# Two modulation matrices loaded in half-width pieces through two buffers

## The chip, the cores and the metric

The kernel runs on one core of one Trainium2 chip. The metric is the device time of one launch in microseconds (us); smaller is better. Engines are named as the profile names them: PE is TensorE (PEld its weight loads), DVE VectorE, ACT ScalarE, POOL GpSimd, SP the queue that issues most DMA loads.

## What is computed

Two transformer blocks run over the same 256 tokens of width 1024. Only the first block's beginning matters here: one vector `c` makes six modulation vectors of 1024 columns by one product with a 1024 x 6144 matrix `ada_w`, and these scale and shift the tokens around the mixer and the mixture of experts.

```python
mod = (jax.nn.silu(c.astype(F32)) @ ada_w.astype(F32) + ada_b.astype(F32)).astype(x.dtype)
sh1, sc1, g1, sh2, sc2, g2 = [m[:, None, :] for m in jnp.split(mod, 6, axis=-1)]
h = rms_norm(x, norm1_g) * (1 + sc1) + sh1
z = h @ w_in
...
attn = dsa_sparse_attention(hs(q), hs(k), hs(v), iq.reshape(B, S, IDX_HEADS, IDX_DIM), ik, iw, rel_bias)
rw = rwkv7_branch(zr, ...)
mixed = jax.nn.sigmoid(ga) * (attn @ w_attn_br) + jax.nn.sigmoid(gr) * (rw @ w_rwkv_br)
x = x + g1 * (mixed @ w_out)
h2 = rms_norm(x, norm2_g) * (1 + sc2) + sh2
x = x + g2 * moe_ffn(h2, ...)
```

## The kernel before

The program is one stream of work for one core, in stages: the first mixer (until about 345 us), the mixture of experts (until about 950 us), and the second block (until the end). A scheduler sets the order of the instructions on every engine, from priorities and from a model of durations of its own; on the chip each engine then runs its queue strictly in that order, and an instruction that waits holds up all behind it. A DMA issue on SP waits there, too.

`modulation(K, g, ...)` makes the modulation vectors in three groups `g` of 2048 columns. Each group runs over eight steps `k` of 128 rows of `ada_w`: a load of 128 x 2048 numbers (1024 KB, 8 KB for each partition), then four products, one for each quarter `q` of 512 columns. The moving side is 512 columns of the weights, the stationary side is `c` copied to 32 columns, and the four quarters go to rows 0, 32, 64 and 96 of one PSUM bank (`mod`), so that the four products lie side by side in the array. In the trace each of them is two records. After eight steps DVE adds the bias (L919, out to the tile `modr`).

Group 0 is needed at once and runs at the start through the wide ring of weight tiles. Groups 1 and 2 are needed only near the end of the mixer. `first_mixer` issues them behind the projection of the rwkv inputs, inside `K.later(400)`, which sets their priorities back, so that they fill in between other work. Their loads have a pool of their own, `ada`, with one buffer `adaw` of 8 KB per partition: the load of step k+1 can be issued only when the last product of step k has read the buffer.

Around them run, on PE: the dense projections of the mixer (`dense_T` and `dense_tok`, three products for each pair of tiles, L186 to L188, weights `w` from `in_w_in_dram` through a ring of three tiles, loaded by L142 and split into a high and a low part by ACT L152 and DVE L153); the chunked rwkv recurrence in two halves (`rwkv`: L1145, L1156, L1133, L1193 to L1271), a long chain between PE, ACT and DVE; the indexer's scores (`dsa_choose`: L1317, read by ACT L1320); and the attention over chosen keys (`dsa`: L543, L583, L555). Sigmoid gates (L1432, L1438) close the mixer, and then the output projections with `w_rwkv_br`, `w_attn_br` and `w_out` follow. ACT loads a function table when it changes between sigmoid and exponential.

Of the kernel before, what the change touches and what calls it, by code (L numbers as in the profile page):

```python
# [893 lines left out]
def modulation(K, g, pool, wpool=None):  # L894

    nc, a = K.nc, K.a
    if g == 0:
        sc = K.t([128, 8], "silc")
        nc.scalar.activation(sc, K.cc["c"], AF.Sigmoid)
        nc.vector.tensor_mul(sc, sc, K.cc["c"])  # L900
        K.c32 = K.t([128, 8, 32], "c32")
        nc.vector.tensor_copy(K.c32, sc[:, :, None].to_broadcast([128, 8, 32]))
        K.modr, K.mrow = {}, {}
    mb = K.modr[g] = K.t([128, 512], "modr", 2, pool=pool)
    v = a["ada_b"][0, g * 2048:g * 2048 + 2048]
    nc.scalar.dma_start(mb, bass.AP(v.tensor, v.offset, [[512, 4], [0, 32], [1, 512]]))
    b = K.bank("mod")
    for k in range(8):
        if g == 0:
            w = K.wtile()  # L910
        else:
            w = K.t([128, 2048], "adaw", pool=wpool)
        nc.sync.dma_start(w, a["ada_w"][0, k * 128:k * 128 + 128, g * 2048:g * 2048 + 2048])
        for q in range(4):
            nc.tensor.matmul(b[32 * q:32 * q + 32], K.c32[:, k], w[:, q * 512:q * 512 + 512], start=(k == 0),
                             stop=(k == 7), skip_group_check=True)
        if k < 7:
            yield
    nc.vector.tensor_add(mb, b, mb)  # L919
    if g:  # L920
        K.mrow[g] = K.dram.tile([4, 512], F32, name="modrow%d" % g)
        nc.scalar.dma_start(K.mrow[g], K.modr[g].rearrange("(q r) n -> q r n", r=32)[:, 0])
    yield
# [436 lines left out]
def first_mixer(K):  # L1360
# [8 lines left out]
    for i, _ in enumerate(modulation(K, 0, first)):  # L1369
        if i == 3:  # L1370
            nc.sync.dma_start(K.X, a["x"][0].rearrange("(h p) d -> p h d", p=128))
# [3 lines left out]
    with K.scope("p1in"):  # L1375
# [20 lines left out]
        with K.later(400), K.after(K.ACT):  # L1396
            for g in (1, 2):
                for _ in modulation(K, g, first, adap):
                    pass
            with K.stream(pool=first, tmp="mod"):  # L1400
                router_in(K, first)
# [752 lines left out]
```

## Time and profile before

| | before |
|---|---|
| median of 3 runs | 1708.5 us (1707.46 to 1713.28) |
| the profiled execution | 1706.39 us, of which the span from first to last instruction is 1704.4 us |
| PE busy | 1620.0 us, 95% of the span |
| DVE, ACT, POOL busy | 829.3, 644.9, 84.8 us |
| mean granted TensorE clock | 0.981 of full speed |
| loads of `adaw` | 16 of 1024 KB, issued from 91.7 to 227.7 us |
| products on `adaw` | 128 records, from 97.8 to 234.5 us |

A line of the time line of an engine gives the start, the length, the engine, the line of the kernel, the operation, the tiles (out<-in), the shape, and how many equal instructions in a row it stands for; in brackets stands the idle time before it and what ended it. Records of matmuls overlap, since they are pipelined: what one costs is read from the start of the next.

### The profile page before, as it was taken

The numbers are of one execution on the slowest core, as the hardware profiler recorded it, in microseconds if no ns is written. First come the engines' busy times: TensorE is split into PE (matmuls) and PEld (weight loads), VectorE is DVE, ScalarE is ACT, GpSimd is POOL, SyncE is SP. The second block draws the span as 40 slices with busy tenths as digits, with TensorE's granted clock in tenths as the row PEclk, the third lists the DMA queues.
The fourth block names the chain that finished last, engine by engine and source line by source line (L and its number), as shares of the span: only waits on it lengthen the run. The fifth ranks groups of instructions, "written<-read, shape, count | busy, mean of one in ns | idle before, by whom it ended". The sixth has DMA issues, their size and how long they took to land. (4 is left out here: it accounts for less than half of the span.)

```text
span 1704.4 us, 28908 instructions
## 1 busy us (share of the span) xinstructions
PE 1620.0 (95%) x11910; PEld 1234.2 (72%) x11910; DVE 829.3 (49%) x1534; ACT 644.9 (38%) x1093; POOL 84.8 (5%) x105
## 2 busy tenths in 40 slices
PE   5999999998989999999999899999999999999997
PEld 2967667786547565557665587889998876989996
DVE  2664786676211321211211356666555677665554
ACT  2432444553121111120111347565444455554443
POOL 2000000103000000000000111211000000000000
PEclk9989899999999999999999999999999999999999
DMA  9454651774999999999999652546555533445551
GB/s 357 151 198 149 206 173 52 276 293 166 414 417 411 390 402 413 412 414 411 393 416 410 198 173 96 191 154 201 193 181 196 175 125 106 143 154 191 197 182 55
DMA packets 138321, 419.06 MB, mean 246 GB/s; under 512 B 10666, under 2 KB 17588, under 8 KB 118732
## 3 DMA queue, kind: packets, MB, share of 16 engines
q1 hardware_dynamic: 126272, 396.39, 62.5%
q0 software_dynamic: 4336, 12.34, 2.2%
q10 hardware_dynamic: 7580, 8.47, 1.7%
q8 instruction: 94, 1.54, 0.4%
q14 instruction: 39, 0.32, 0.1%
HBM read 410.88 MB, written 6.32 MB: 245 GB/s over the span
## 5 line engine op out<-in xcount | busy, mean ns | idle before, releaser
L153 DVE TENSOR_TENSOR w<-w 128x1024 fp32r<-128x1024 f32 (+1 forms) x283 | 347.5, 1229 | 260.8 <-ACT w L152 260.0
L152 ACT ACTIVATE w<-w 128x1024 fp32r<-128x1024 f32 (+1 forms) x285 | 299.9, 1054 | 315.7 <-PE acc L188 223.4
L1897 PE MATMUL tmp<-w 128*32 128x256 f32 (+2 forms) x2560 | 202.1, 396 | 14.9 <-DMA w<-in_exp_up_dram 10.0
L1897 PEld LDWEIGHTS tmp<-w 128*32 128x32 f32 (+2 forms) x2560 | 120.6, 122 | 87.4 <-DMA w<-in_exp_up_dram 13.3
L188 PE MATMUL acc<-hTh,w 128*128 128x256 f32 (+2 forms) x552 | 159.4, 289 | 1.1 <-DVE w L153 1.1
L186 PE MATMUL acc<-hTh,w 128*128 128x256 f32 (+2 forms) x552 | 158.0, 287 | 1.8 <-ACT w L152 1.1
L187 PE MATMUL acc<-hTl,w 128*128 128x256 f32 (+2 forms) x552 | 159.0, 288 | 0.2 <-DVE hTl L153 0.2
L186 PE MATMUL tmp<-hTh,w 128*128 128x256 f32 x512 | 143.6, 280 | 0.0
L187 PE MATMUL tmp<-hTl,w 128*128 128x256 f32 x512 | 143.0, 279 | 0.0
L188 PE MATMUL tmp<-hTh,w 128*128 128x256 f32 x512 | 142.9, 279 | 0.0
L188 PEld LDWEIGHTS acc<-hTh,w 128*128 128x128 f32 (+1 forms) x552 | 105.5, 191 | 6.6 <-issue 4.6
L187 PEld LDWEIGHTS acc<-hTl,w 128*128 128x128 f32 (+1 forms) x552 | 105.7, 192 | 5.1 <-issue 4.1
L186 PEld LDWEIGHTS acc<-hTh,w 128*128 128x128 f32 (+1 forms) x552 | 105.7, 192 | 4.7 <-issue 2.0
L1925 PE MATMUL tmp<-w,fT 128*32 128x512 f32 (+2 forms) x640 | 105.2, 597 | 0.5 <-ACT fT L1913 0.5
L186 PE MATMUL acc<-w,gh 128*128 128x512 f32 x256 | 100.0, 390 | 0.0
L188 PE MATMUL acc<-w,gl 128*128 128x512 f32 x256 | 99.8, 390 | 0.0
L187 PE MATMUL acc<-w,gh 128*128 128x512 f32 x256 | 99.6, 389 | 0.0
L186 PEld LDWEIGHTS tmp<-hTh,w 128*128 128x128 f32 x512 | 96.1, 188 | 0.5
L188 PEld LDWEIGHTS tmp<-hTh,w 128*128 128x128 f32 x512 | 96.3, 188 | 0.0
L187 PEld LDWEIGHTS tmp<-hTl,w 128*128 128x128 f32 x512 | 95.8, 187 | 0.5
L1903 DVE SCALAR_TENSOR_TENSOR ff<-tmp,gsl,fs 128x256 f32<-128x256 f32 x26 | 12.6, 483 | 171.6 <-ACT fs L1901 171.6
L1901 ACT ACTIVATE fs<-tmp 128x256 f32<-128x256 f32 x26 | 10.0, 385 | 217.9 <-PE tmp L1897 217.9
(625 smaller groups left out, 2884.4 us busy)
## 6 DMA issues: line engine op xcount, KB each, us to landing
w<-in_exp_gate_dram SPq DMA_DIRECT2D x64, 1024.0 KB, 18.2
w<-in_exp_up_dram SPq DMA_DIRECT2D x64, 1024.0 KB, 18.7
w<-in_exp_down_dram SPq DMA_DIRECT2D x64, 1024.0 KB, 15.4
w<-in_mlp_w_dram SPq DMA_DIRECT2D x64, 1024.0 KB, 5.2
w<-in_w_in_dram SPq DMA_DIRECT2D x23, 1024.0 KB, 6.2
adaw<-in_ada_w_dram SPq DMA_DIRECT2D x16, 1024.0 KB, 5.2
w<-in_xa_wkv_dram SPq DMA_DIRECT2D x16, 1024.0 KB, 20.5
w<-in_sb_w_in_dram SPq DMA_DIRECT2D x12, 1024.0 KB, 5.2
```

Of the source, the lines that this page charges most:

```text
L152: self.nc.scalar.activation(hi, src, AF.Copy)
L153: self.sub.tensor_tensor(lo, src, hi.bitcast(F32), op=OP.subtract)
L186: mm(out, lh, rh, start=first, stop=False, skip_group_check=True)
L187: mm(out, lh, rl, start=False, stop=False, skip_group_check=True)
L188: mm(out, ll, rh, start=False, stop=last, skip_group_check=True)
L1897: nc.tensor.matmul(b[at:at + w, x * 256:x * 256 + 256], X[:, k, i * 128 + at:i * 128 + at + w], d[n][:, k], start=(x == 0 and k == 0), sto ...
L1901: nc.scalar.activation(s, b[:, 0:256], AF.Silu)
L1903: nc.vector.scalar_tensor_tensor(f, b[:, 256:512], g, s, op0=OP.mult, op1=OP.mult)
L1925: nc.tensor.matmul(b[at:at + w], fT[:, k, at:at + w], d["exp_down"][:, k, n * 512:n * 512 + 512], start=(k == 0), stop=(k == 1), skip_grou ...
```

## The change

For groups 1 and 2 a step of 128 rows is cut into two halves of columns. There are 16 loads `i` for each group; `k` is the row step, `n` the half. A load brings columns `n*256` to `n*256 + 256` of each of the four quarters, 128 x 4 x 256 numbers (512 KB, four pieces of 1 KB for each partition). The pool `ada` now has two such buffers of 4 KB per partition, so its size stays as it was. Each half has four products of 256 columns into its half of the bank. Group 0 is as it was.

```diff
     b = K.bank("mod")
-    for k in range(8):
-        if g == 0:
-            w = K.wtile()
-        else:
-            w = K.t([128, 2048], "adaw", pool=wpool)
+    for i in range(16 if g else 0):
+
+        k, n = divmod(i, 2)
+        c = slice(n * 256, n * 256 + 256)
+        w = K.t([128, 4, 256], "adaw", 2, pool=wpool)
+        nc.sync.dma_start(w, a["ada_w"][0, k * 128:k * 128 + 128, g * 2048:g * 2048 + 2048]
+                          .rearrange("p (q c) -> p q c", q=4)[:, :, c])
+        for q in range(4):
+            nc.tensor.matmul(b[32 * q:32 * q + 32, c], K.c32[:, k], w[:, q], start=(i == 0), stop=(k == 7),
+                             skip_group_check=True)
+        yield
+    for k in range(0 if g else 8):
+        w = K.wtile()
         nc.sync.dma_start(w, a["ada_w"][0, k * 128:k * 128 + 128, g * 2048:g * 2048 + 2048])
```

Since the scheduler sets the order, the change moves more than its own lines. Lines behind the change have numbers higher by 8 in the changed kernel (L1133 is L1141, the products L915 are L916).

On the queue of SP, from the first load of `adaw` on, before (`w<-in_w_in_dram` are the weights of the projections):

```order
L913 DMA adaw<-in_ada_w_dram 128x2048 x2
L142 DMA w<-in_w_in_dram 128x4x512
L913 DMA adaw<-in_ada_w_dram 128x2048
L142 DMA w<-in_w_in_dram 128x4x512
L913 DMA adaw<-in_ada_w_dram 128x2048 x2
L142 DMA w<-in_w_in_dram 128x4x512
L913 DMA adaw<-in_ada_w_dram 128x2048 x3
L142 DMA w<-in_w_in_dram 128x4x512
```

and in the changed kernel, the whole of it:

```order
L913 DMA adaw<-in_ada_w_dram 128x4x256 x6
L142 DMA w<-in_w_in_dram 128x4x512
L913 DMA adaw<-in_ada_w_dram 128x4x256 x2
L142 DMA w<-in_w_in_dram 128x4x512
L913 DMA adaw<-in_ada_w_dram 128x4x256 x14
L142 DMA w<-in_w_in_dram 128x4x512
L913 DMA adaw<-in_ada_w_dram 128x4x256 x6
L142 DMA w<-in_w_in_dram 128x4x512
L913 DMA adaw<-in_ada_w_dram 128x4x256 x4
L142 DMA w<-in_w_in_dram 128x4x512 x8
```

Fourteen loads of `adaw` in a row now stand ahead of a load of projection weights, and the last load of `adaw` stands ahead of eight of them, where before it stood ahead of four.

On PE in the middle of the first rwkv half (L1133 are its 64 x 64 products), before:

```order
L1133 MATMUL rw<-rP,rWT 64x64 x8
L186 MATMUL acc<-hTh,w 128x256
L187 MATMUL acc<-hTl,w 128x256
L915 MATMUL mod<-adaw,c_104 32x512
L1133 MATMUL rw<-rWT,rP 64x64 x8
L1133 MATMUL rw<-rP,rWT 64x64 x8
L915 MATMUL mod<-adaw,c_104 32x512 x3
L188 MATMUL acc<-hTh,w 128x256
L186 MATMUL acc<-hTh,w 128x256
```

and at the same place in the changed kernel:

```order
L1141 MATMUL rw<-rP,rWT 64x64 x8
L916 MATMUL mod<-adaw,c_104 32x256 x4
L188 MATMUL acc<-hTh,w 128x256
L1141 MATMUL rw<-rWT,rP 64x64 x8
L1141 MATMUL rw<-rP,rWT 64x64 x8
L916 MATMUL mod<-adaw,c_104 32x256 x4
L186 MATMUL acc<-hTh,w 128x256
L1141 MATMUL rw<-rW,rlm 64x64 x16
L1141 MATMUL rw<-rWT,rP 64x64 x8
L1141 MATMUL rw<-rP,rWT 64x64 x8
L916 MATMUL mod<-adaw,c_104 32x256 x4
```

A half step now stands behind nearly every second run of rwkv products, and dense products that filled these places have moved back. Over the whole queue of PE the products on `adaw` stand in 38 runs, where they stood in 21, and the last of them stands right behind the indexer's scores instead of in the second rwkv half.

## Rows read from the trace of the kernel before

**Rows 1.** The page, busy time by engine and its share of the span.

```profile
PE 1620.0 (95%) x11910; PEld 1234.2 (72%) x11910; DVE 829.3 (49%) x1534; ACT 644.9 (38%) x1093; POOL 84.8 (5%) x105
```

**Rows 2.** Stretches: length, busy time of each engine (instructions), granted clock, DMA share, GB/s.

```profile
97.00:197.00 100.00, 94.62 (x986) 67.17 (x985) 58.90 (x133) 34.36 (x66) 2.04 (x2) 0.94 0.53 178
197.00:240.00 43.00, 41.57 (x234) 28.84 (x233) 38.84 (x102) 21.89 (x36) 0.00 (x0) 0.99 0.55 192
240.00:312.00 72.00, 71.67 (x779) 53.26 (x779) 51.42 (x130) 32.43 (x77) 6.03 (x9) 1.00 0.27 83
```

**Rows 3.** Groups of PE from 80 to 245 us: busy, mean ns, idle before.

```profile
L915 PE MATMUL mod<-adaw,c 128*32 128x512 f32 x128 | 23.1, 633 | 3.5 <-DMA adaw<-in_ada_w_dram 3.5
```

**Rows 4.** Time line of PE, products on adaw and those around them.

```profile
97.34 0.28 PE L186 MATMUL acc<-hTh,w 128*128 128x256 f32 x1
97.78 1.06 PE L915 MATMUL mod<-adaw,c 128*32 128x512 f32 x8 [0.16 <-DMA adaw<-in_ada_w_dram]
98.77 0.39 PE L187 MATMUL acc<-hTl,w 128*128 128x256 f32 x1
99.00 0.28 PE L188 MATMUL acc<-hTh,w 128*128 128x256 f32 x1
99.12 0.28 PE L186 MATMUL acc<-hTh,w 128*128 128x256 f32 x1
...
126.51 1.05 PE L915 MATMUL mod<-adaw,c 128*32 128x512 f32 x2
127.49 1.15 PE L1133 MATMUL rw<-rW,rlm 64*64 64x64 f32 x32
128.72 0.68 PE L1133 MATMUL rw<-rWT,rP 64*64 64x64 f32 x16
129.23 0.63 PE L1133 MATMUL rw<-rP,rWT 64*64 64x64 f32 x16
129.79 1.06 PE L915 MATMUL mod<-adaw,c 128*32 128x512 f32 x6
130.78 0.39 PE L186 MATMUL acc<-hTh,w 128*128 128x256 f32 x1
```

**Rows 5.** Time line of PE, the two other products on adaw that waited.

```profile
192.38 1.94 PE L915 MATMUL mod<-adaw,c 128*32 128x512 f32 x8 [2.29 <-DMA adaw<-in_ada_w_dram]
...
219.68 1.06 PE L915 MATMUL mod<-adaw,c 128*32 128x512 f32 x8 [1.08 <-DMA adaw<-in_ada_w_dram]
```

**Rows 6.** Time line of PE among the expert products, a run on 32 columns.

```profile
569.60 5.60 PE L1897 MATMUL tmp<-w 128*32 128x256 f32 x100
```

**Rows 7.** Time line of SP, issues of loads.

```profile
91.66 7.58 SPq L913 DMA_DIRECT2D adaw<-in_ada_w_dram  x2
...
135.77 0.38 SPq L142 DMA_DIRECT2D w<-in_w_in_dram  x1
...
184.28 10.42 SPq L913 DMA_DIRECT2D adaw<-in_ada_w_dram  x2
...
211.95 0.33 SPq L913 DMA_DIRECT2D adaw<-in_ada_w_dram  x1
```

**Rows 8.** Issues of two loads: engine, count, KB each, median us to landing.

```profile
adaw<-in_ada_w_dram SPq DMA_DIRECT2D x16, 1024.0 KB, 5.2
...
memx<-memkv ACTq DMA_DIRECT2D x16, 256.0 KB, 3.7
```

**Rows 9.** Stretches of 5 us around the longest wait; columns as in the second group.

```profile
185.00:190.00 5.00, 4.13 (x25) 2.12 (x22) 4.11 (x12) 3.58 (x9) 0.00 (x0) 0.79 1.04 361
190.00:195.00 5.00, 2.71 (x11) 0.70 (x10) 1.95 (x6) 2.24 (x4) 0.00 (x0) 0.50 0.22 65
195.00:200.00 5.00, 5.00 (x30) 4.61 (x29) 2.44 (x4) 1.98 (x4) 0.00 (x0) 0.69 0.60 210
```

**Rows 10.** Time line of PE: the values' projection begins, attention ends, w_rwkv_br begins.

```profile
203.74 0.39 PE L186 MATMUL acc<-w,hTh 128*128 128x512 f32 x1
203.97 0.39 PE L187 MATMUL acc<-w,hTh 128*128 128x512 f32 x1
...
307.46 0.86 PE L555 MATMUL tmp<-pT,av__232 128*64 128x256 f32 x6
...
329.11 0.40 PE L186 MATMUL acc<-w 128*128 128x512 f32 x1
```

**Rows 11.** Groups of ACT until 340 us, a table load.

```profile
L1432 ACT ACT_TABLE_LOAD x2 | 2.6, 1283 | 0.0
```

## The prediction

> **What bounds the kernel now.** I read the busy times first: PE is busy 95% of the span, the next engine 49% [rows 1]. Then the stretches in which groups 1 and 2 of the modulation run. From 97 to 197 us PE is busy 94.62 of 100 us, DVE 58.90; from 197 to 240 us PE 41.57 of 43 us and DVE 38.84, so there the two are nearly level; from 240 to 312 us PE 71.67 of 72 us [rows 2]. The stage is bound by PE's queue, which runs strictly in order, and time is saved or lost by what that queue holds and by what it waits for. The third view is the group of the products on `adaw`: 128 records, busy 23.1 us, and an idle time of only 3.5 us before them [rows 3]. That idle time is all that a second buffer can give back directly, 0.2% of the span. The waits behind it are three: 0.16 us at 97.78, 2.29 us at 192.38 and 1.08 us at 219.68 [rows 4, 5]. The issue queue shows why: the load after the products of one step is issued at once (184.28 and 211.95 us [rows 7]) and its products start 8.1 and 7.7 us later. At all other steps the scheduler has put enough other work between.
>
> **The change, part by part.** It removes nothing from the work: the same bytes are loaded and the same columns multiplied.
>
> First, the products. A whole step costs 0.99 us from its start to that of the next instruction (97.78 to 98.77). A quarter alone (two records) costs as much, 126.51 to 127.49, because the four quarters run side by side [rows 4]. For 256 columns on 32 rows of output the trace has the expert products: 100 records in 5.60 us, so eight in 0.45 us [rows 6]. Two halves are 0.90 us, and so 0.09 us of a step is the edge of a run. A half in a run of its own costs 0.45 + 0.09 = 0.54 us. Amid dense products a run also costs a change at both ends: 97.34 to 97.78 is 0.44 us, less 0.16 us of waiting and the 0.12 us that dense products stand apart (99.00 to 99.12), so 0.16; and 98.77 to 99.00 is 0.23, less 0.12, so 0.11 [rows 4]; 0.27 us together. Beside rwkv products this change is paid anyway. Before, the order has 21 runs, 5 of them amid dense products: 21 x 0.99 + 5 x 0.27 = 22.1 us, near the busy time of the group, which holds some steps at the lower clock [rows 3]. Now it has 38 runs, two of them holding a further half's worth, 8 amid dense products: 38 x 0.54 + 2 x 0.45 + 8 x 0.27 = 23.6 us. So the products cost **+1.5 us**. If a half has no edge of its own (0.45) it is -1.9 us, with twice the edge (0.64) it is +5.3 us; the trace has no lone half of this shape. I take the middle, since a lone quarter shows that a run's edge does not shrink with what it holds.
>
> Second, the waits. With two buffers, a half's load is issued when the products of the half two before it have ended. What counts is the PE work between those two points, against the time from issue to start. Along the new order, at the durations of the old trace, I get 30 such gaps. An example from the order shown, first run to third: a dense product 0.12, the two rwkv pairs 1.07 (128.72 to 129.79), a half 0.54, a dense product 0.12, sixteen rwkv products 1.23 (127.49 to 128.72), a pair 1.07 [rows 4]: 4.2 us. The gaps run from 2.9 us (the last half of the indexer's scores and the one after) to 7.3 us; twelve are under 4.3 us. The old order's 15 gaps run from 3.8 to 8.3 us, against a whole load.
>
> The time from issue to start of a 512 KB load is not in the trace. The nearest are 3.7 us to landing for 256 KB and 5.2 us for 1024 KB [rows 8]; on the line between them 512 KB take 4.2 us. Start comes somewhat after landing (97.78 - 91.66 = 6.1 us at the first wait [rows 4, 7], against the median of 5.2 us [rows 8]); I add 0.3 us and take 4.5 us. Adding up, in order, what each gap falls short of that, and letting each wait lengthen the gap beside it, gives 7 us of waits; 3.6 us at 4.0, 9.7 us at 4.8, 18 us at 5.5. The same sum for the old order, with 5.2 + 0.3 us, gives 4.6 us where 3.5 us was measured [rows 3], since the real queue is a little slower than its parts. I scale by that, 0.76: 5.3 us of new waits, less the 3.5 us that go: **+1.8 us**. The bounds are 2.7 us (4.0) and 14 us (5.5): -0.8 and +10.5 us.
>
> A rule of the Trainium skill speaks against this part: its page DMA: Bandwidth & Descriptors (Bandwidth, and the fit in Anatomy of one DMA) says that a transfer pays about 2.0 us whatever its size and should be 1 MiB or more. The fit gives 4.4 us for 1024 KB, where this trace shows 5.2 us [rows 8], and 3.2 us for 512 KB, a step of 1.2 us between the two sizes; taken from 5.2 us it would put the start at 4.3 us and the sum 0.8 us lower than mine.
>
> Third, what is moved. Sixteen more issues on SP cost nothing on the path: SP only issues. But the projection weights now stand behind runs of six to fourteen `adaw` loads, each of which waits for PE. The nearest to its use is the first half of the values' weights: issued at 135.77 us [rows 7], first used at 203.74 us [rows 10]. In the new order it follows the load that waits for the 19th half, about 165 us, so some 40 us of cover are left where it needs about 5. If that cover were gone, each such load would cost its landing, about 5 us; I cost it at nothing. The dense products that are pushed back, and the five steps that now come before the indexer's end, are work exchanged for work. They start the indexer's selection, the attention and the second rwkv half some 8 to 12 us later within a PE queue of nearly the same length. The cover: attention's last products end at 308.3 us, and the product with `w_rwkv_br` begins at 329.11 us [rows 10], 21 us. In the new order 92 dense products of 512 columns, 0.23 us apart (203.74 to 203.97), stand between the last attention scores and the first product that reads the attention: again about 21 us. ACT gets four more table loads, 4 x 1.28 = 5.1 us [rows 11], at 32.43 of 72 us busy [rows 2]; nothing unless PE waits for a bank. Clock: no change taken.
>
> **The sum**: +1.5 + 1.8 = +3.3 us on the profiled execution's 1706.4 us, 1709.7 us. The median of the runs is 2.1 us above that execution, so the time for a median is 1708.5 + 3.3, about **1712 us**. About 0.3%, 5 us, is what a measurement of this kernel can tell from no change; this is inside it.
>
> **The rivals.** (a) *A half takes as long to land as a whole.* It has 512 pieces of 1 KB where the whole has 128 of 8 KB; if the number of pieces or the latency sets the time, issue to start is 5.5 us and PE waits at 18 of 30 halves: 14 - 3.5 + 1.5 = +12 us, **1720 us**, slower. It decides from 4.8 us on, where waits pass 7 us and the sum passes 5 us. For it: a quarter of the bytes saves only 1.5 of 5.2 us [rows 8]. Against: 256 KB of memx do land faster.
>
> (b) *The late chain.* DVE at 90% from 197 to 240 us [rows 2] now starts its selection 8 to 12 us later, and ACT has four more table loads; if in-order PE meets attention or rwkv products whose inputs aren't there, it stands. For it: that occupancy. Against: the 21 us of cover, and PE at over 99% from 240 to 312 us. One switch of 1.28 us ahead of each of four head pairs' exponentials plus the same lag on DVE: about +5 more, **1717 us**, slower.
>
> (c) *The waits go, and the low clock with them.* At the longest wait the granted clock falls to 0.79, 0.50 and 0.69 in three stretches of 5 us [rows 9]: busy time times what is missing is 4.13 x 0.21 + 2.71 x 0.50 + 5.00 x 0.31 = 3.8 us. If a half lands like memx (3.7 us, start at 4.0), the waits are 2.7 us, and if this dip goes too, the sum is 1.5 - 0.8 - 3.8 = -3 us, and with halves that have no edge -6.5 us: **1703 us**, faster. Against: the indexer's scores themselves stutter there, and four short gaps stand among or behind them in the new order.
>
> **How the numbers follow.** Forecast 0.50, (a) 0.25, (b) 0.12, (c) 0.13. Same is the forecast, slower (a) and (b), 0.37, faster (c). The range reaches from (c), 1703 us, to a little above (a), 1722 us; turnarounds beyond 5.5 us lie outside.
>
> **What would show it.** In the changed trace: landings of 512 KB near 4.2 us; idle before the products on `adaw` near 5 us, spread over some ten short waits, most at the indexer's scores; products starting 0.54 us before the next instruction; the granted clock between 185 and 200 us; PE idle for DVE or ACT from 240 to 330 us under 1 us. Landings above 4.5 us, or PE waiting for attention, would make the prediction wrong upward; a clock at 1.00 through the indexer downward.

## The result, and the profile after

The changed kernel takes 1719.1 us in the median of 4 runs (1714.68 to 1721.71), against 1708.5 us: the ratio is 1.0054 with a 95% interval of 1.0037 to 1.0071. Measured again (11 runs) it was 1.0061 (1.0039 to 1.0083). It is slower by about 0.6%, some 10 us. The forecast was 1712 us and "within 0.3%"; the time lies in the range, and it came out on the slower side, with 0.37.

The profiled execution took 1714.68 us. Nearly all of its loss arises in the mixer. The transposes of the mixed branches (L243, tile `mx`, the first work behind the branch products) begin at 355.0 us where they began at 347.3 us; from there to the end the difference stays at 7.7 to 8.5 us (the spans are 1704.4 and 1712.9 us).

The group of the products on `adaw`, to set beside [rows 3] (columns: busy, mean ns, idle before), and PE's waits for these loads (us in total, times, longest):

```profile
L916 PE MATMUL mod<-adaw,c 128*32 128x256 f32 x256 | 27.6, 436 | 9.0 <-DMA adaw<-in_ada_w_dram 9.0
```
```profile
PE mod L916 <- DMA adaw<-in_ada_w_dram: 9.0, 7, 4.2
PE tmp L1325 <- ACT ixr L1328: 1.1, 1, 1.1
```

The idle time before the products grew from 3.5 to 9.0 us, though each load is half as large and has a second buffer. The page's line of the loads, beside [rows 8]:

```profile
adaw<-in_ada_w_dram SPq DMA_DIRECT2D x32, 512.0 KB, 3.8
```

A half lands in 3.8 us in the median, where 4.2 was forecast. The trace holds a landing for only 15 of the 32 halves, and for three of the 16 whole loads behind the 5.2 us of [rows 8]. The median says little of the late halves:

```profile
DMA to landing us min/median/max: 3.6/3.8/8.2
```

The time line of PE, beside [rows 4, 5], has these waits (in brackets the idle time and what ended it):

```profile
97.58 1.08 PE L916 MATMUL mod<-adaw,c 128*32 128x256 f32 x8 [4.18 <-DMA adaw<-in_ada_w_dram]
98.59 0.58 PE L188 MATMUL acc<-hTh,w 128*128 128x256 f32 x1
...
115.67 0.64 PE L916 MATMUL mod<-adaw,c 128*32 128x256 f32 x8 [0.74 <-DMA adaw<-in_ada_w_dram]
116.24 0.39 PE L188 MATMUL acc<-hTh,w 128*128 128x256 f32 x1
...
186.64 0.64 PE L916 MATMUL mod<-adaw,c 128*32 128x256 f32 x8 [1.01 <-DMA adaw<-in_ada_w_dram]
...
191.01 0.64 PE L916 MATMUL mod<-adaw,c 128*32 128x256 f32 x8 [0.55 <-DMA adaw<-in_ada_w_dram]
197.92 0.65 PE L916 MATMUL mod<-adaw,c 128*32 128x256 f32 x4 [2.05 <-DMA adaw<-in_ada_w_dram]
```

Without the first, the waits sum to 4.8 us; 5.3 us were forecast, most of it where it is, among the indexer's scores (186 to 198 us). The first, 4.18 us, was not in the forecast at all.

The longest of the others, 2.05 us at 197.92, is a wait for the load that SP issued at 189.68 us (a row stands for three issues; the first starts there), 8.2 us earlier, while the DMA engines were busy throughout (share 1.04, 377 GB/s):

```profile
189.68 9.75 SPq L913 DMA_DIRECT2D adaw<-in_ada_w_dram  x3
```
```profile
190.00:195.00 5.00, 3.24 (x35) 1.63 (x29) 4.08 (x12) 2.82 (x6) 0.00 (x0) 1.00 1.04 377
```

At its longest wait the kernel before needed 8.1 us from the issue of a whole load to the start of its products (184.28 to 192.38 [rows 5, 7]). So where PE waits longest, a half came no sooner than a whole.

At the full clock a lone half costs 0.57 us (115.67 to 116.24), where 0.54 was forecast; at 97.58 it costs 1.01 us. The clock tells why. Stretches of 5 us of the changed kernel (length, busy time of PE, PEld, DVE, ACT and POOL, granted clock, DMA share, GB/s), beside [rows 9]:

```profile
85.00:90.00 5.00, 5.00 (x27) 2.97 (x26) 1.15 (x2) 2.14 (x5) 0.51 (x1) 1.00 0.74 249
90.00:95.00 5.00, 3.40 (x20) 2.12 (x18) 4.54 (x12) 3.82 (x6) 0.00 (x0) 1.00 0.67 185
95.00:100.00 5.00, 2.42 (x14) 1.61 (x15) 3.28 (x5) 2.25 (x4) 0.00 (x0) 0.68 0.53 163
100.00:105.00 5.00, 5.00 (x29) 3.77 (x28) 0.00 (x0) 0.00 (x0) 0.00 (x0) 0.64 0.65 201
105.00:110.00 5.00, 5.00 (x36) 3.10 (x34) 4.19 (x10) 2.17 (x3) 0.00 (x0) 0.70 0.33 105
```

and of the kernel before, where the first product waited 0.16 us [rows 4]:

```profile
85.00:90.00 5.00, 5.00 (x14) 2.82 (x12) 0.76 (x2) 1.43 (x3) 0.52 (x1) 0.55 0.70 247
90.00:95.00 5.00, 5.00 (x24) 3.05 (x24) 2.33 (x5) 2.27 (x4) 0.00 (x0) 0.77 0.56 185
```

So the executions differ in the course of the clock ahead of the first product, on work that the change does not touch. Two readings were open: that the wait belongs to the new order, whose first product stands 14 dense products earlier, or that it belongs to the execution. The experiments had to tell what the loss of 10 us is made of: products, waits, moved work, or clock.

### The profile page after: what moved, and what is told of

It is laid out like the page before. It is cut to its first block, busy times and chain, and to the rows that moved or that the text cites. A ratio compares the mean times of both kernels' runs of the same rounds, so it can differ in the third digit from the quotient of the medians.

```text
span 1712.9 us, 29201 instructions
## 1 busy us (share of the span) xinstructions
PE 1624.4 (95%) x12038; PEld 1238.6 (72%) x12038; DVE 829.0 (48%) x1534; ACT 649.2 (38%) x1097; POOL 85.4 (5%) x105
```

## The experiments

Times are medians of 11 or 12 runs, ratios are against runs of the kernel before on the same chip.

**Products of 256 columns alone.** Whole loads, one buffer.

```diff
-        for q in range(4):
+        for n in range(2 if g else 0):
+            for q in range(4):
+                c = slice(n * 256, n * 256 + 256)
+                nc.tensor.matmul(b[32 * q:32 * q + 32, c], K.c32[:, k], w[:, q * 512 + n * 256:q * 512 + n * 256 + 256],
+                                 start=(k == 0 and n == 0), stop=(k == 7), skip_group_check=True)
+        for q in range(0 if g else 4):
...
```

> The kernel before with its whole loads of 1024 KB and its one buffer, but eight products of 256 columns for a step instead of four of 512: the narrower products alone. The order keeps nearly its shape (22 runs of products instead of 21), so no step is cut into halves that stand apart. Theory (the loss of the changed kernel is 2.7 us of products, because 38 runs each have an edge, and 5.5 us of waits for loads): here the edges are as before, so the time is within 1.5 us of the kernel before, and the idle time before the products stays between 3 and 5 us. Rival (256 columns are dearer in themselves, as the busy time of the group in the changed kernel, 27.6 us against 23.1 us, may be read): 4 to 5 us slower with the same idle time.

Measured: 1705.8 us, ratio 0.9982 (0.9968 to 0.9996): if anything faster (2.1 us, a little outside the 1.5 us of the theory). The idle time before the products is 3.4 us. Narrower products are not dear in themselves. The time line of PE in this kernel shows what they can save:

```profile
138.88 0.62 PE L917 MATMUL mod<-adaw,c 128*32 128x256 f32 x2
139.43 0.56 PE L1138 MATMUL rw<-rWT,rP 64*64 64x64 f32 x12
```

Two records of 256 columns cost 0.55 us. In the kernel before, a part of a step in a run of its own costs 0.98 us, nearly a whole step (126.51 to 127.49 [rows 4]), and five of its steps are cut in two.

**Two loads of 512 KB into one buffer.** The order on PE is that of the kernel before.

```diff
-        nc.sync.dma_start(w, a["ada_w"][0, k * 128:k * 128 + 128, g * 2048:g * 2048 + 2048])
+        if g == 0:
+            nc.sync.dma_start(w, a["ada_w"][0, k * 128:k * 128 + 128, g * 2048:g * 2048 + 2048])
+        else:
+            v = a["ada_w"][0, k * 128:k * 128 + 128, g * 2048:g * 2048 + 2048]
+            for n in range(2):
+                nc.sync.dma_start(w.rearrange("p (q c) -> p q c", q=4)[:, :, n * 256:n * 256 + 256],
+                                  v.rearrange("p (q c) -> p q c", q=4)[:, :, n * 256:n * 256 + 256])
```

> The kernel before, but every load of 1024 KB for groups 1 and 2 is made as two loads of 512 KB into the same buffer, in the form that the changed kernel uses (four pieces of 1 KB for each partition). The order of the instructions on TensorE is the same as before, instruction for instruction, so that only the loads differ. Theory (a load of 512 KB lands in 3.8 us since size counts, and two overlap): the pair is in after about 5.2 us as the whole was, the idle time before the products stays at 3 to 5 us, and the time is within 1.5 us of the kernel before. Rival (512 pieces of 1 KB are slow in themselves, each load pays its time behind the other): the second lands after some 7.6 us, nearly every step waits, and the idle time before the products grows to 15 us or more, the time by as much.

Measured: 1709.8 us, ratio 1.0002 (0.9984 to 1.0020). The loads' form costs nothing that can be measured; in pairs they land in 4.9 us in the median. The profiled execution was the slowest of its twelve (1718.2 us); its first product waited 3.8 us, in the order of the kernel before. That was the first sign that this wait needs no new order.

**One half buffer instead of two.** The changed kernel with one number changed.

```diff
-        w = K.t([128, 4, 256], "adaw", 2, pool=wpool)
+        w = K.t([128, 4, 256], "adaw", 1, pool=wpool)
```

> The changed kernel with one buffer of half the columns instead of two, so that a half's load is issued only when the half before it has been read. The scheduler makes 34 runs of it and puts them further apart, the last one some 370 matrix instructions later. Theory (waits for loads go one for one into the time): the work between two halves is often 2 to 4 us against 3.8 us of landing, so the idle time before the products is 10 to 20 us instead of 9, and the time is longer than that of the changed kernel by about what this idle time grows, 1 to 11 us. Rival (the changed kernel lost its time through what was moved, not through the waits: here the order stays nearer to the one before, and the last products stand later, not earlier): the time comes back toward the kernel before, within 4 us of it, whatever the idle time is.

Measured: 1711.3 us, ratio 1.0020 (1.0004 to 1.0035), clearly less than the changed kernel. Expected were more waits. The scheduler puts the steps further apart (the last product starts at 275.7 us, in the changed kernel at 207.8 us), and the waits are these:

```profile
PE mod L916 <- DMA adaw<-in_ada_w_dram: 4.7, 6, 1.5
```

This execution had the low clock at 85 to 95 us (0.59 and 0.73), and its first product did not wait. So its 4.7 us are to be set against the 4.8 us behind the first product in the changed kernel, not against all 9.0: the second buffer bought no shorter waits, since the scheduler spent it on standing the halves closer. The theory (a longer time) falls. The rival's number held, within 4 us of the kernel before, but what brought the time back this run does not show.

**The router's weights out of the way** (the load moved to another queue, ahead of the first `adaw` load).

```diff
+        K.wr = K.t([128, 8, 64], "wr", pool=first)
+        nc.gpsimd.dma_start(K.wr, a["router_w"][0].rearrange("(k p) n -> p k n", p=128))
...
-    w = K.t([128, 8, 64], "wr")
-    nc.scalar.dma_start(w, a["router_w"][0].rearrange("(k p) n -> p k n", p=128))
-    K.wr = w
+    w = K.wr
```

> The changed kernel with the load of the router's weights (128 x 8 x 64 numbers in pieces of 256 bytes) issued on GpSimd's queue before the first load for groups 1 and 2, instead of on ScalarE's queue beside it. The order of the products shifts a little (36 runs instead of 38). Theory (the first wait of the changed kernel, 4.18 us at 97.58 us, is made longer by that load, which lies on the same DMA engines): the first half lands in about 4 us instead of 5 and that wait falls to 2 to 3 us; the time falls by 1 to 2 us against the changed kernel. Rival (the wait comes from the place of the first products alone, 14 dense products earlier than before): the wait stays at 4 us and the time within 0.7 us.

Measured: 1714.4 us, ratio 1.0032 (1.0017 to 1.0048). Its profile has the low clock at 85 to 95 us (0.64 and 0.67) and no wait at the first product, so it says nothing on that wait; the interval touches those of the changed kernel, and the order differs too. Inconclusive.

**The changed kernel again.** Unchanged.

> The changed kernel once more, for a second profile and more times. The profiles so far differ in where the granted clock first falls: at 85 to 95 us in the kernel before and in the changed kernel with one half buffer, at 95 to 110 us, behind an idle time of 3.4 to 4.2 us at the first product, in the changed kernel and in the kernel before with narrower products or with two loads for a step. Theory A (the first wait of 4.18 us belongs to the execution: with a full clock TensorE is early and waits for the load, with a low clock it comes when the load is there): the second profile may show either, and where it shows the early fall, the first wait is under 1 us and the idle time of the group 5 to 6 us; the time is that of the first measurement, 0.3 to 0.7% slower than before. Theory B (the wait belongs to the order, whose first product stands 14 dense products earlier): the wait of about 4 us is there again.

Measured: 1718.2 us (1712.38 to 1727.91), ratio 1.0061. The profiled execution (1723.63 us) waits at the first product again, and more behind it. PE's group, and its time line:

```profile
L916 PE MATMUL mod<-adaw,c 128*32 128x256 f32 x256 | 28.5, 444 | 12.0 <-DMA adaw<-in_ada_w_dram 12.0
```
```profile
98.02 1.08 PE L916 MATMUL mod<-adaw,c 128*32 128x256 f32 x8 [4.08 <-DMA adaw<-in_ada_w_dram]
...
115.65 1.08 PE L916 MATMUL mod<-adaw,c 128*32 128x256 f32 x8 [3.13 <-DMA adaw<-in_ada_w_dram]
...
207.22 1.08 PE L916 MATMUL mod<-adaw,c 128*32 128x256 f32 x8 [2.23 <-DMA adaw<-in_ada_w_dram]
```

SP issued the sixth half just before 108.3 us (the end of this row; a row stands for six issues), and its products start at 115.65 us, over 7 us later:

```profile
92.58 15.70 SPq L913 DMA_DIRECT2D adaw<-in_ada_w_dram  x6
109.63 0.37 SPq L142 DMA_DIRECT2D w<-in_w_in_dram  x1
```

Beside it lie others. The issues from 104 to 120 us (KB each, median us to landing):

```profile
adaw<-in_ada_w_dram SPq DMA_DIRECT2D x4, 512.0 KB, 4.2
w<-in_w_in_dram SPq DMA_DIRECT2D x2, 1024.0 KB, 8.6
t5b<-t_scratch ACTq DMA_DIRECT2D x2, 128.0 KB, 6.7
```

The median of 4.2 us hides such a half. Behind this wait comes a fall of the clock that no other profile has between 110 and 180 us:

```profile
110.00:115.00 5.00, 2.52 (x20) 1.50 (x18) 4.67 (x8) 0.00 (x0) 0.00 (x0) 0.97 0.93 268
115.00:120.00 5.00, 4.35 (x21) 3.14 (x22) 1.56 (x2) 1.57 (x3) 0.00 (x0) 0.50 0.83 284
120.00:125.00 5.00, 5.00 (x22) 3.07 (x21) 2.44 (x5) 0.24 (x1) 0.00 (x0) 0.50 0.64 213
125.00:130.00 5.00, 5.00 (x13) 2.69 (x11) 0.69 (x1) 0.00 (x0) 0.00 (x0) 0.50 0.33 105
130.00:135.00 5.00, 5.00 (x33) 3.03 (x32) 2.45 (x6) 0.98 (x3) 0.00 (x0) 0.50 0.29 84
135.00:140.00 5.00, 5.00 (x77) 3.60 (x77) 3.32 (x7) 2.57 (x5) 0.00 (x0) 0.98 0.08 24
```

For some 20 us the granted clock is 0.50, the 1.2 GHz level, with PE busy: (4.35 + 3 x 5.00) x 0.50 = 9.7 us lost. Four of the 11 runs, this one among them, lie at 1723.6 to 1727.9 us, the other seven at 1712.4 to 1718.3 us; where the other three lost their time no profile shows, but each run's mean granted clock is on record. It is 0.972 to 0.974 in these four and 0.977 to 0.982 in the other seven, and no run of any other kernel here lies under 0.975.

**The first two halves later.** The rest of the order hardly moves (35 runs).

```diff
-        for q in range(4):
...
+        with K.later(300 if g == 1 and i < 2 else 0):
+            for q in range(4):
...
```

> The changed kernel with the priority of the products of its first two halves set back by another 300, so that they stand 51 matrix instructions later, as one run of eight; 35 runs instead of 38, the rest of the order nearly the same. Theory B (the first wait belongs to the place of the first product): the first wait goes, the idle time of the group falls from 9 to about 5 us and the time by about 4 us against the changed kernel. Theory A (it belongs to the execution, where a full clock turns into a wait): the time falls by no more than the three runs saved, under 1.5 us. Rival (what was moved costs, not the waits): no difference either, and the idle time has gone.

Measured: 1710.6 us, ratio 1.0018 (1.0003 to 1.0033), no interval in common with the changed kernel: 7.6 us of its 10 us are gone. More than the first wait of 4 us, so none of the three expectations had its size. In its profile the clock was full until 95 us, as in the changed kernel; the first product (100.23 us) waits for nothing, the waits at 107 and 108 us are 0.54 and 0.82 us, and no fall of the clock follows at 115 us. PE's waits for these loads:

```profile
PE mod L917 <- DMA adaw<-in_ada_w_dram: 6.8, 6, 2.4
```

**No loads behind the first two.** The products read the same two halves.

```diff
+        if g == 1 and i < 2:
             w = K.t([128, 4, 256], "adaw", 2, pool=wpool)
...
+            K.aw = [w] if i == 0 else K.aw + [w]
+        w = K.aw[n]
```

> The changed kernel with only the first two halves loaded; all 32 halves read these two buffers, so that 30 loads and all waits for them are left out, and with them the right values of groups 1 and 2. The scheduler then makes 19 runs and ends them 290 matrix instructions earlier. Theory (the loss is waits for loads and edges of runs): only the first wait can be left; against the changed kernel 5 to 9 us of waits and 19 runs of 0.1 us go, so the time is 1709 to 1713 us at most, and lower where dense products are no longer parted. Rival (products that stand earlier push the rwkv, indexer and attention work back, and that is the loss): it stays as slow as the changed kernel or becomes slower, 1718 us or more, with TensorE idle for VectorE or ScalarE instead.

Measured: 1702.4 us, ratio 0.9966 (0.9949 to 0.9983), 16 us below the changed kernel and below what the theory gave. (It leaves out 30 loads, and the right values with them.) It ends the products earlier than any other kernel here, and so moves the most work back; the rival of the moved work falls. Its only wait for a load is at the first product:

```profile
PE mod L919 <- DMA adaw<-in_ada_w_dram: 4.4, 1, 4.4
```

It is as long as in the changed kernel, in the kernel with the shortest time of all. So the first wait by itself is not what makes a kernel slow.

**Only the first step halved.** The first products stand where the changed kernel has them, all else is as before.

```diff
+        if g == 1 and k == 0:
+            for n in range(2):
+                c = slice(n * 256, n * 256 + 256)
+                h = w[:, n * 1024:n * 1024 + 1024].rearrange("p (q c) -> p q c", q=4)
+                nc.sync.dma_start(h, a["ada_w"][0, 0:128, 2048:4096].rearrange("p (q c) -> p q c", q=4)[:, :, c])
+                for q in range(4):
+                    nc.tensor.matmul(b[32 * q:32 * q + 32, c], K.c32[:, k], h[:, q], start=(n == 0), stop=False,
+                                     skip_group_check=True)
+            yield
+            continue
```

> The kernel before with one change: the first step of group 1 is loaded as two loads of 512 KB into its buffer, with four products of 256 columns each; the other fifteen steps are as before. In the order the first products now stand 14 dense products earlier, at the place that they have in the changed kernel, and the rest is nearly as before (22 runs instead of 21). Theory (the early place of the first product costs its wait of 4.1 us and is the largest part of the loss): the first product waits about 4 us, the time is 4 to 8 us longer than before, 1712 to 1716 us. Rival (the loss of the changed kernel lies in its other 36 runs): within 2 us of the kernel before, with or without the wait.

Measured: 1707.4 us, ratio 0.9979 (0.9963 to 0.9994). The wait is there, and the loss is not, as the rival had it:

```profile
96.95 1.08 PE L919 MATMUL mod<-adaw,c 128*32 128x256 f32 x8 [4.39 <-DMA adaw<-in_ada_w_dram]
97.96 0.58 PE L188 MATMUL acc<-hTh,w 128*128 128x256 f32 x1
```

My theory that the early place is the largest part of the loss falls.

**The kernel before again.** Unchanged.

> The kernel before, unchanged, for a second profile. Every profile so far belongs to one of two courses: the granted clock falls at 85 to 95 us and the first product finds its load there, or the clock stays full until 95 us, the first product waits 3.4 to 4.4 us, and the fall comes at 95 to 110 us. Theory (the course belongs to the execution, not to the order or the loads): if this profile has a full clock at 85 to 95 us, the first product waits 3 to 4 us here too, so that this wait is no cost of the change; its time is then 1709 us or more. If it has the early fall, it repeats the first profile (wait under 0.5 us) and the point rests on the other kernels. Rival (the whole loads of the kernel before never leave a wait there): full clock at 85 to 95 us and a wait under 1 us. In both courses no fall of the clock at 110 to 180 us, which only the second profile of the changed kernel has.

Measured: ratio 0.9998 (0.9983 to 1.0012); the profiled execution, 1707.9 us, took the other course:

```profile
85.00:90.00 5.00, 5.00 (x28) 2.96 (x27) 1.31 (x2) 1.96 (x5) 0.52 (x1) 1.00 0.74 247
90.00:95.00 5.00, 5.00 (x35) 3.92 (x34) 4.36 (x12) 3.85 (x5) 0.00 (x0) 1.00 0.68 182
95.00:100.00 5.00, 1.78 (x14) 0.74 (x14) 3.47 (x5) 2.41 (x4) 0.00 (x0) 1.00 0.41 160
100.00:105.00 5.00, 5.00 (x34) 4.47 (x33) 2.96 (x8) 2.02 (x3) 0.00 (x0) 0.87 0.59 210
```
```profile
98.45 1.07 PE L915 MATMUL mod<-adaw,c 128*32 128x512 f32 x8 [3.22 <-DMA adaw<-in_ada_w_dram]
```

The unchanged kernel waits 3.22 us at its first product when the clock was full ahead of it, and 0.16 us when it was low [rows 4]; the times of the two executions differ by 1.5 us. The load is issued when a ring of buffers comes free, 91.7 to 92.6 us in all four profiles of the two kernels; in these executions the full clock before that only turned into a wait. The expected 1709 us or more for this course was wrong: it cost next to nothing.

**Three tries for a faster kernel.** First whole loads and products of 256 columns as in the first experiment, the priority set back by less (18 runs of products):

```diff
-        with K.later(400), K.after(K.ACT):
+        with K.later(200), K.after(K.ACT):
```

> The kernel before with its whole loads and one buffer, eight products of 256 columns for a step as in the first experiment, and the priority of both groups set back by 200 instead of 400, which makes 18 runs of products instead of 22. Theory (each run has an edge of about 0.1 us and amid dense products 0.27 us more; narrower products cost nothing more): the time is that of the first experiment or up to 2 us less, 1703 to 1706 us, faster than both kernels. Rival (the gain of the first experiment, 0.18%, was chance or came of its order): within 1 us of the kernel before.

Measured: 1705.3 us, ratio 0.9984 (0.9968 to 0.9999), inside the theory's range, by an interval that nearly reaches 1. The same line alone, in the kernel before, with its products of 512 columns (18 runs):

```diff
-        with K.later(400), K.after(K.ACT):
+        with K.later(200), K.after(K.ACT):
```

> The kernel before with nothing changed but the priority of both groups, set back by 200 instead of 400: whole loads, products of 512 columns, 18 runs instead of 21. It is to be set against the same with products of 256 columns (0.9984 of before). Theory (a part of a step in a run of its own costs 0.55 us with 256 columns and 0.97 us with 512, and in the kernel before five steps were cut in two): with the cuts mostly gone the time is 1 to 3 us below before, near that of the narrower products. Rival (256 columns are cheaper in themselves): the same time as before.

Measured: 1704.8 us, ratio 0.9984 (0.9968 to 0.9999), with no wait for a load left:

```profile
L915 PE MATMUL mod<-adaw,c 128*32 128x512 f32 x128 | 20.9, 662 | 0.0
```

With fewer steps cut in two, the width no longer matters, as the theory had it. Last, 256 columns again and a smaller number:

```diff
-        with K.later(400), K.after(K.ACT):
+        with K.later(100), K.after(K.ACT):
```

> As the fastest kernel so far (whole loads, one buffer, products of 256 columns), with the priority set back by 100: 17 runs, of which all but one hold a whole step. Theory (edges of runs and waits are what is left): 0 to 2 us faster than with 200, so 1703 to 1706 us. Rival (nothing is left there to save, and products that stand earlier meet their loads): the same or 1 to 3 us slower, with more idle time before the products than 1.6 us.

Measured: 1705.3 us, ratio 0.9973 (0.9960 to 0.9986), faster than both kernels by its interval, though not apart from the others of these tries: that nothing was left to save there, as the rival had it, fits. Its first product waits 3.84 us, where the same order up to there with `K.later(200)` waited 0.20 us: again the course of the clock.

## Why the prediction was right in part and wrong in part

To set the profiles side by side I split the time from 80 us to the first transpose of `mx` (L243) in three: PE's idle time, the clock (in each stretch of 5 us, busy time times what the granted clock lacks from 1), and what remains, the work at the full clock.

| execution | its time | stretch | idle | clock | work |
|---|---|---|---|---|---|
| before, first | 1706.4 | 267.3 | 7.6 | 8.9 | 250.8 |
| before, second | 1707.9 | 268.1 | 10.6 | 5.6 | 251.9 |
| changed, first | 1714.7 | 275.0 | 12.7 | 8.5 | 253.8 |
| changed, second | 1723.6 | 286.2 | 15.2 | 18.1 | 253.0 |
| one half buffer | 1707.9 | 267.0 | 7.9 | 8.1 | 251.0 |
| first halves later | 1708.4 | 266.8 | 11.2 | 6.6 | 249.1 |
| first step halved | 1709.8 | 273.3 | 13.9 | 8.6 | 250.8 |
| no reloads | 1699.4 | 260.1 | 8.6 | 6.4 | 245.1 |

Mean against mean, the changed kernel has 4.9 us more idle time, 6.0 us more lost to the clock and 2.0 us more work. The two executions of each kernel differ by more than some of these numbers, so the sizes are rough, and of the clock the profiles alone cannot say that it grew: the changed kernel's first lost no more to it (8.5 us) than the first of before (8.9 us).

The runs say more, since each has its span and its mean granted clock (to 0.001, 1.7 us of one run) on record. Span times what the clock lacks from 1 is what the clock took, here with idle time included; the rest is the span without it. Means in us, all from the chip of the second measurement:

| kernel | runs | taken by the clock | the rest |
|---|---|---|---|
| before | 34 | 33.2 | 1673.6 |
| changed | 11 | 39.5 | 1677.9 |
| changed, the four longest runs | 4 | 46.1 | 1677.6 |
| changed, the other seven | 7 | 35.7 | 1678.0 |
| first halves later | 12 | 37.8 | 1671.7 |
| no reloads | 12 | 33.2 | 1667.3 |

So of a loss of 10.5 us in the mean about 6 us are the clock's (give or take 1.8 us, one standard error) and about 4 us are products, waits and other idle time (give or take 0.7 us), for which +3.3 us were forecast. The four long runs differ from the other seven by the clock alone.

*Products, +1.5 us forecast.* Right: work grew by 1.1 to 3.0 us, and a lone half costs 0.57 us where 0.54 was taken. The price of runs also explains much of the shortest time: by the prediction's own prices 32 halves in 19 runs (32 x 0.45 + 19 x 0.09 = 16.1 us) cost 5 us less than in 38 (38 x 0.54 + 2 x 0.45 = 21.4 us), without the changes amid dense products; the work of the kernel without reloads is 8 to 9 us less. What the rest is no run shows.

*Waits, +1.8 us forecast.* The mechanism was right, and the size fits one profile of two. Behind the first product the waits are 4.8 us in one profile and 7.9 us (12.0 less 4.08) in the other, against 5.3 forecast; before they are 3.4 [rows 4, 5] and 3.3 us. The term I sized badly is the time from issue to start: one value, 4.5 us, was taken for all 30 gaps. Many halves land in 3.6 to 5 us, but the longest waits belong to single late halves: 2.05 us at 197.92 to a half that landed after 8.2 us, and in the second profile 2.23 us at 207.22 to one that landed after 8.8 us and 3.13 us at 115.65 to one that was over 7 us from issue to start. My rows had this already: at the two waits of before a whole load took 8.1 and 7.7 us from issue to start, and I took 5.5 us, from a median over three landings.

A rule of the Trainium skill (DMA: Bandwidth & Descriptors, Anatomy of one DMA) gives 3.2 us for 512 KB by its fit, which the page has from loads issued by GpSimd; these are issued by SP. An estimate from it alone would have made the waits smaller still. The traces do not agree: no half landed in under 3.4 us in the two profiles, and single ones in over 8 us.

*The first wait, taken as 0.16 us.* One profile of the kernel before was read as its property. In the same course of the clock the first wait is 3.22 us before and 4.1 to 4.2 us after: the change adds 0.9 us there, not 4.

*Clock, taken at nothing.* This is the step that failed. Over the runs the clock took about 6 us more than before, more than products and waits together. In the profiles it is -0.4 or +2.9 us in the first (against the two of before) and +9.2 or +12.5 us in the second, 9.7 us of it lost in one fall behind the wait at 115.65 us. I had looked at the clock only for what might be won back (rival c), at the longest wait of before.

What brings the fall on stays open. The new order puts six halves between 97 and 117 us where two steps stood, so two waits can lie 18 us apart; with the first two halves set back the first wait is gone, the next are 0.54 and 0.82 us, the profile has no such fall, and none of the 12 runs has a mean clock under 0.976. That speaks for the pair of waits. But over those runs the clock still takes 4.6 us more than before and only 1.7 us less than in the changed kernel (give or take 2 us); of what comes back there, 6.2 us are in the rest. And the changed kernel's first profile has two such waits, of 4.18 and 0.74 us, and no such fall. So the pair of waits as the cause is a guess from one profile, not shown.

*Moved work at nothing.* No run speaks against it: where the products ended earliest, the time was shortest, though that kernel has fewer loads and fewer runs of products too. PE's waits for VectorE and ScalarE moved (the indexer's scores now wait 1.4 us for ScalarE, 0.9 before; waits of the rwkv products of 0.9 and 0.8 us are gone) but their sum is 3.1 us, 3.3 before.

*The rivals.* (a) named 1720 us for halves that land as slowly as a whole, with PE waiting at 18 of them: near the time by luck, since PE waited for seven and six, though the halves at the longest waits were as slow as a whole. (b) named 1717 us for a late chain, and PE did not wait for it. (c) had the sign of the clock the wrong way round. The range held because the bounds of the waits were wide, not because the clock was foreseen, and that is luck; the chance of 0.50 for "same" was too high, since a term that one profile cannot show was set at zero.

## What to carry to other kernels

Here the scheduler used a second buffer to stand the readers closer together, and then the real landing times, those of the late loads beside others and not the median, set the waits: fewer and wider steps were better than a second buffer. Before one landing time is taken for all loads, read issue to start at the waits that the trace already has. Where one engine bounds the time, a change of its order can cost more by the clock than by its waits, so that term must not be set at zero; the granted clock of every run tells it better than one profile. Before a wait is counted as a kernel's own, look at more than one execution: the 3 to 4 us at the first product came and went in the same kernel at nearly equal time.

## What the runs showed of the hardware

A load half as large took little less from issue to start: at the first product 5.4 to 5.5 us (with the next half in flight beside it) instead of 6.1 to 6.2 us, and at the longest wait behind it 8.2 us against 8.1 us, with the DMA engines busy throughout for 5 us of each (share 1.04 at 185 us before [rows 9] and at 190 us after). Products on 32 columns of output that lie side by side cost together what one of them costs: a lone quarter of 512 columns 0.98 us, a whole step of four 0.99 us; a lone quarter of 256 columns 0.55 us, four 0.57 us. The granted clock fell to the 1.2 GHz level for some 20 us, behind 3.13 us of waiting and with PE busy from 115.65 us on, and was back at 0.98 in the stretch of 135 to 140 us. And executions of one kernel differ in their clock: the same order lost 35.7 us to it in seven runs and 46.1 us in four.
